# The last gate's weight rows spread more thinly over the MLP, and loaded two ahead instead of three in its second product

## The chip, the cores and the metric

The kernel runs on one core of a Trainium2 chip. The metric is the device time of one execution in microseconds, from runs on the chip; 2004.98 us is the median of three runs before the change. One more execution was profiled, and every view below is of that one.

Five engines work side by side, each through its own list of instructions and strictly in that list's order as far as this text is concerned: PE (matrix multiplication), DVE and ACT (elementwise work), POOL (here it mostly issues DMAs) and SP (it issues most DMAs). An instruction that has to wait holds everything behind it on its own engine.

## The reference, cut to what matters

One decoder layer on 512 tokens of width 2048. A conditioning vector `c` gives six modulation vectors; the sixth, `gt2`, gates the output of the MLP:

```
mod = (c_act @ w_ada[l] + b_ada[l]).reshape(B, N_MOD, D)
sh1, sc1, gt1, sh2, sc2, gt2 = [mod[:, j][:, None, :] for j in range(N_MOD)]
...
h = rmsnorm(x, g_norm_mlp[l]) * (1.0 + sc2) + sh2
hid = jnp.square(jax.nn.relu(jnp.einsum('bsd,df->bsf', h, w_mlp_in[l])))
y = jnp.einsum('bsf,fd->bsd', hid, w_mlp_out[l])
x = (x + gt2 * y)
...
return rmsnorm(x, g_norm_final)
```

`gt2` depends only on `c` and `w_ada`, so it can be computed at any time before the first finished column block of the second product is multiplied by it. `w_mlp_in` is 2048 x 8192 and `w_mlp_out` 8192 x 2048, all in float32.

## The kernel before, in words

The core first computes attention, the recurrence and their output product (up to about 780 us), and then the MLP, which is the rest.

**The MLP's two products.** Both are done as Strassen-like block products (`strassen`, L1079): seven products of blocks (`PRODUCTS`, L1073) are summed in seven PSUM banks, and `combine` (L1110 to L1117) adds and subtracts the seven banks to four result blocks. A *chunk* is one step of the inner loop: one 512 KB block of weights and 42 matmuls (L1099, L1100, L1101, 128x128 by 128x256). A *set* is the chunks that sum into the same seven banks. The first product has 15 sets of 8 chunks (g = 1 to 15; I number its chunks 0 to 119). The second has 124 chunks of this kind, 120 to 243, in 13 `parts`. PSUM has 8 banks, which the sets take in turn, so a set's first chunk finds one bank free, and the six others as soon as `combine` of the set before has read them.

**What a chunk needs.** `operands` (L1048) loads the weight block on SP into one of three `raw` buffers (L1055) and prepares it: DVE adds parts of it (L1057, L1064, L1065, into `ts`), ACT rounds both to a high part (L1063 and L1069), and DVE subtracts to get the low parts (two L122 subtractions, `w<-raw,w` with 768 columns and `w<-ts,w` with 1024). PE multiplies by the high and the low part. The buffers `w` come free when PE has done with them.

**Beside the chunks** of the first product, `keep_parts` squares and stores the four results of the set before (POOL stores at L937 and L946) for the second product. In the second, `load_pair` (L1138 `a<-part`, L1141 `a<-sum`, on SP) brings them back, `split_pair` (ACT L1148, DVE L122) splits the sums, and at the end of a part the seven banks are copied out and stored by POOL (L1289, `prod<-a`), or combined.

**The rows.** `ada_late(GT2)` (L1185) computes the gate: 64 *rows*, each a 128x512 quarter of a row block of `w_ada`, 256 KB. For each: SP loads it (L1189; the order of these loads in SP's list is kept as written), DVE multiplies it by the conditioning vector and sums along it (L1200, `SCALAR_TENSOR_TENSOR` and the `DVE_READ_ACCUMULATOR` that comes with it), and after each fourth two tiny DVE operations finish a piece (L1205, L1206). The rows run as a background job that starts with g = 2. It is paced: each chunk gives one tick, and the job goes on by one row per `pace[0]` ticks. If it is not done when the gate is first needed (`ensure(GT2)`, before the first finished column block, 108 chunks into the second product), the rest is emitted at once there. While the first product is written, the rows use the buffers `n` (5 of them, `row[0] = "n"`); from the second product on `a` (64 of them), which are also those of `load_pair` and of the copies that POOL stores.

The order of each engine's list is set by a scheduler from the order in the program and from priorities: the loads and preparations of `operands` are raised by 200 places (`SETW`), `combine` by 330 (`SETE`). So a change of the background's pace also shifts where the neighbours of a row stand.

Of the kernel before, what the change touches and what calls it, by code (L numbers as in the profile page):

```python
# [19 lines left out]
NK = D // P  # L20
# [44 lines left out]
def hybrid_layer_kernel(  # L65
# [32 lines left out]
    def T(tag, dt=F32, cols=None):  # L98
        return new(next(split_tag) if tag == "w4" else tag, dt, cols)
# [48 lines left out]
    def col(base, j):  # L148
        return vec[:, base + j : base + j + 1]
# [29 lines left out]
    def later(ins):  # L179
        return tc.keep_in_program_order(ins)  # L180


    def mod(m, j):
        return mods[:, m * NK + j : m * NK + j + 1]

    class Rows:
# [6 lines left out]
        def load(self, n, tags):  # L193
            queue = nc.sync if tags is MID else nc.sync if tags is LATE else nc.sync
            for _ in range(n):
                if self.todo and tags:
                    i, q = self.todo.pop(0)
                    t = T(next(tags))[:, :1024]
                    later(queue.dma_start(t, w_adaT[i * P : (i + 1) * P, q * 1024 : (q + 1) * 1024]))
                    self.tiles[i, q] = t  # L200
# [68 lines left out]
    class Lane:  # L269
# [8 lines left out]
        def next(self):  # L278
            if not self.queue:
                return False  # L280
            try:
                self.wait += next(self.queue[0]) or 0.0
            except StopIteration:
                self.queue.pop(0)
            return True
# [421 lines left out]
    pace = [3.2]  # L707
# [463 lines left out]
    todo = {}  # L1171
# [11 lines left out]
    LEAD, row = 3, ["n"]  # L1183

    def ada_late(m):  # L1185

        def load(i):
            t = T(row[0])
            tc.keep_in_program_order(nc.sync.dma_start(t, w_adaT[(m * NK + i // 4) * P : (m * NK + i // 4 + 1) * P, i % 4 * S : (i % 4 + 1) * S]))  # L1189
            return t  # L1190

        ts = [load(i) for i in range(LEAD)]
        for i in range(4 * NK):
            t, q = ts.pop(0), i % 4
            if i + LEAD < 4 * NK:
                ts.append(load(i + LEAD))
            yield pace[0]
            if q == 0:
                ga = T("ga")
            stt(  # L1200
                out=t, in0=t, scalar=1.0, in1=cb[q // 2][:, q % 2 * S : (q % 2 + 1) * S], op0=ALU.mult, op1=ALU.mult,
                accum_out=ga[:, q : q + 1],
            )
            if q == 3:
                tt(out=ga[:, :2], in0=ga[:, :2], in1=ga[:, 2:4], op=ALU.add)  # L1205
                stt(  # L1206
                    out=mod(m, i // 4), in0=ga[:, 0:1], scalar=ga[:, 1:2], in1=col(C_BADA, m * NK + i // 4),
                    op0=ALU.add, op1=ALU.add,
                )
        ready.add(m)  # L1210

    pace[0] = 1.9
    w_pair = w_mlp_in.rearrange("(c k p) f -> k p c f", c=2, p=P)
    for g in range(1, NG):
        if g == 2:
            bg2.add(ada_late(GT2))
        last = (lambda j: after_set()) if g == NG - 1 else None
        bs = strassen(lambda j: w_pair[j][:, :, g * 512 : (g + 1) * 512], acts_in, last, js=range(KP)[:: -1 if g == 1 else 1])
        with tc.high_priority(offset=SETE):
            r = [T("a") for _ in range(4)]  # L1220
            q11, q12, q22, q21 = combine(bs, *r)

            rs = q12, q11, q21, q22
        bg.add((keep_parts if g < NG - 2 else hold_parts)(g, *rs))
# [235 lines left out]
```

## Time and profile before

| | before |
|---|---|
| median of 3 runs | 2004.98 us (2004.24 to 2006.26) |
| the profiled execution | 2004.49 us |
| its span, first to last instruction | 2002.8 us |
| PE busy | 1947.9 us, 97% of the span |
| DVE busy | 1761.3 us, 88% |
| ACT busy | 1076.5 us, 54% |
| DMA, mean | 220 GB/s |
| the rows (L1200) | 62 in `n` from 836.4 to 1357.5 us, 2 in `a` from 1410.5 to 1414.5 us |

The first product of the MLP (chunks 0 to 119) ends at about 1356 us; the second product runs from there to the end. In a window of 40 us in which PE never waits, 355 or 356 matmuls are counted. A matmul's busy time (0.28 us) is more than the distance between two of them, since they overlap; the count per window tells the pace, and the busy time only when PE stood still. A few matmul records can be missing, so a count that is 2 short with a busy time of 40.00 is no loss.

### The profile page before, as it was taken

To read this page: it belongs to the slowest core of one execution; us is meant where nothing else is said; L and a number is where in the kernel's file an instruction comes from. 1 tells how busy PE (TensorE), PEld (TensorE's weight loads), DVE (VectorE), ACT (ScalarE), POOL (GpSimd) and SP (SyncE) were. 2 spreads that over 40 slices of the span, in tenths; PEclk is the share of its full clock that TensorE was granted. 3 is DMA by queue.
4 is the path that set the end of the run, shared out by engine and by line. 5 is a ranking of instruction groups with operands and counts; after the bars stand their busy time and mean duration, and the time that the engine had idled before them with its cause. 6 is when DMAs were issued, how large, how long until landed. Compare 5 with 4: busy or idle time off the path is not lost. (4 is left out here: it accounts for less than half of the span.)

```text
span 2002.8 us, 37929 instructions
## 1 busy us (share of the span) xinstructions
PE 1947.9 (97%) x14532; PEld 1837.3 (92%) x14532; DVE 1761.3 (88%) x2971; ACT 1076.5 (54%) x1572; POOL 181.2 (9%) x283
## 2 busy tenths in 40 slices
PE   8999999999999998999999999999999999999997
PEld 6789898788888898999999999999999999999996
DVE  8998786878998599999999999999879879788986
ACT  4443564786533385555555556556445545555542
POOL 0000000000000000112111211200110210210000
PEclk9999999999999999999999999999999999999998
DMA  9896655556779544766666666755577667677644
GB/s 364 303 318 215 207 167 184 181 150 215 226 250 369 170 139 138 233 196 213 217 193 208 227 195 193 228 177 195 185 250 252 247 246 273 229 254 272 235 148 153
DMA packets 205624, 441.45 MB, mean 220 GB/s; under 512 B 20353, under 2 KB 41985, under 8 KB 205442
## 3 DMA queue, kind: packets, MB, share of 16 engines
q1 hardware_dynamic: 178642, 360.78, 54.9%
q0 software_dynamic: 21760, 71.32, 9.5%
q10 hardware_dynamic: 5040, 6.93, 1.0%
q8 instruction: 114, 1.87, 0.4%
q14 instruction: 68, 0.56, 0.1%
HBM read 375.25 MB, written 63.70 MB: 219 GB/s over the span
## 5 line engine op out<-in xcount | busy, mean ns | idle before, releaser
L1099 PE MATMUL ps_mm<-a,w 128*128 128x256 f32 x1696 | 468.8, 277 | 2.3 <-DVE a L1111 1.2
L1101 PE MATMUL ps_mm<-a,w 128*128 128x256 f32 x1696 | 468.9, 277 | 2.1 <-DVE w L122 1.9
L1100 PE MATMUL ps_mm<-a,w 128*128 128x256 f32 x1696 | 468.8, 277 | 0.3 <-DVE a L122 0.3
L1069 ACT ACTIVATE w<-ts 128x1024 fp32r<-128x1024 f32 x244 | 258.8, 1061 | 273.9 <-DVE ts L1065 248.7
L1101 PE MATMUL ps_z<-a,w 128*128 128x256 f32 x1304 | 361.6, 278 | 8.3 <-DVE w L122 8.3
L1099 PE MATMUL ps_z<-a,w 128*128 128x256 f32 x1304 | 361.5, 278 | 3.6 <-DVE a L1115 1.6
L1100 PE MATMUL ps_z<-a,w 128*128 128x256 f32 x1304 | 361.1, 277 | 0.1
L122 DVE TENSOR_TENSOR w<-ts,w 128x1024 fp32r<-128x1024 f32 x244 | 298.6, 1224 | 58.6 <-PE ps_mm L1101 26.5
L1099 PEld LDWEIGHTS ps_mm<-a,w 128*128 128x128 f32 x1696 | 318.6, 188 | 3.6 <-issue 2.5
L1101 PEld LDWEIGHTS ps_mm<-a,w 128*128 128x128 f32 x1696 | 318.9, 188 | 2.9 <-DVE w L122 2.8
L1100 PEld LDWEIGHTS ps_mm<-a,w 128*128 128x128 f32 x1696 | 319.0, 188 | 0.7 <-DVE a L122 0.7
L122 DVE TENSOR_TENSOR w<-raw,w 128x768 fp32r<-128x768 f32 (+1 forms) x296 | 268.5, 909 | 39.0 <-ACT w L244 23.6
L1063 ACT ACTIVATE w<-raw 128x768 fp32r<-128x768 f32 x244 | 204.8, 840 | 169.8 <-issue 85.5
L1101 PEld LDWEIGHTS ps_z<-a,w 128*128 128x128 f32 x1304 | 245.4, 188 | 10.0 <-DVE w L122 9.9
L1099 PEld LDWEIGHTS ps_z<-a,w 128*128 128x128 f32 x1304 | 245.7, 188 | 5.0 <-issue 2.1
L1100 PEld LDWEIGHTS ps_z<-a,w 128*128 128x128 f32 x1304 | 245.8, 189 | 0.6 <-DVE a L122 0.6
L244 ACT ACTIVATE wh<-wr 128x512 fp32r<-128x512 f32 (+1 forms) x184 | 113.4, 620 | 152.3 <-PE ps_mm L262 65.2
L259 PE MATMUL ps_mm<-a,wh 128*128 128x512 f32 x448 | 176.2, 393 | 3.7 <-DVE a L460 1.6
L1057 DVE TENSOR_TENSOR ts<-raw 128x512 f32<-128x512 f32 x244 | 167.8, 688 | 12.8 <-DMA raw<-in_w_mlp_out_dram 11.9
L263 PE MATMUL ps_mm<-a,wl 128*128 128x512 f32 x448 | 175.1, 391 | 0.4 <-DVE wl L122 0.2
L262 PE MATMUL ps_mm<-a,wh 128*128 128x512 f32 x448 | 174.8, 390 | 0.0
L122 DVE TENSOR_TENSOR wl<-wr,wh 128x512 fp32r<-128x512 f32 (+1 forms) x184 | 124.7, 681 | 33.3 <-ACT wh L244 32.5
(332 smaller groups left out, 4154.4 us busy)
## 6 DMA issues: line engine op xcount, KB each, us to landing
raw<-in_w_mlp_out_dram SPq DMA_DIRECT2D x124, 512.0 KB, 4.2
raw<-in_w_mlp_in_dram SPq DMA_DIRECT2D x120, 512.0 KB, 3.9
x<-in_w_adaT_dram SPq DMA_DIRECT2D x108, 512.0 KB, 5.8
wr<-in_w_in_dram SPq DMA_DIRECT2D x160, 256.0 KB, 3.4
tt<-in_w_adaT_dram SPq DMA_DIRECT2D x52, 512.0 KB, 6.5
part<-a POOLq DMA_DIRECT2D x84, 256.0 KB, 3.9
a<-part SPq DMA_DIRECT2D x84, 256.0 KB, 6.4
prod<-a POOLq DMA_DIRECT2D x63, 256.0 KB, 5.8
```

The source lines that it names most:

```text
L122: tt(out=out, in0=full, in1=f32(high), op=ALU.subtract)
L244: act(h[:, :n], r[:, :n], AF.Copy)
L259: first = mm(out, wh, ah, start=start, stop=False, **kw)
L262: mm(out, wh, al, start=False, stop=False, **kw)
L263: mm(out, wl, ah, start=False, stop=stop, **kw)
L1057: tt(out=t[:, : 2 * HT].rearrange("p (a b) -> p a b", a=2), in0=r[:, HT : 3 * HT].rearrange("p (a b) -> p a b", a=2), in1=r[:, q_(0)].unsq ...
L1063: act(h, r[:, HT:], AF.Copy)
L1069: act(h, t, AF.Copy)
L1099: mm(out, wh[:, blk(i)], ah, start=st, stop=False, **kw)
L1100: mm(out, wh[:, blk(i)], al, start=False, stop=False, **kw)
L1101: mm(out, wl[:, blk(i)], ah, start=False, stop=j == js[-1], **kw)
```

## The change

The pace goes from 1.9 ticks per row to 3.2. The loads are kept in a list, `todo`; while the rows use the buffers `n`, three of them are ahead of the row that is computed, as before, and once they use `a`, two.

```diff
-        ts = [load(i) for i in range(LEAD)]
+        todo = list(range(4 * NK))
+        ts = [load(todo.pop(0)) for _ in range(LEAD)]
         for i in range(4 * NK):
             t, q = ts.pop(0), i % 4
-            if i + LEAD < 4 * NK:
-                ts.append(load(i + LEAD))
+            if todo and len(ts) < (LEAD if row[0] == "n" else 2):
+                ts.append(load(todo.pop(0)))
             yield pace[0]
...
-    pace[0] = 1.9
+    pace[0] = 3.2
```

64 rows at 1.9 ticks take 122 ticks, and 112 chunks are left of the first product when the job starts. At 3.2 they take 205 ticks, of 112 + 108 before the gate is needed. In the lists of the engines, DVE's rows stand before: 60 by chunk 113, then one each near chunks 121 and 122, 132 and 133. They stand now: 37 by chunk 112, one at 121, and 26 between chunks 132 and 203. In pieces: six rows at chunks 20 to 24 before and six now, six at 31 to 33 before and two at 31 and 32 now, 34 in the sets from chunk 48 to 111 before and 20 now.

The lists also change around the end of the first product. On ACT, which copies the first of the seven banks of the last set (L1110), before:

```order
1111 L1063 ACTIVATE w_2731_15908<-raw_15904 128x768
1112 L1069 ACTIVATE w_2733_15914<-ts_15906 128x1024
1113 L1063 ACTIVATE w_2742_15981<-raw_15977 128x768
1114 L1110 ACTIVATE a_15766<-ps_z_15224 128x512
1115 L1069 ACTIVATE w_2744_15987<-ts_15979 128x1024
```

and after:

```order
1111 L1063 ACTIVATE w_2701_15818<-raw_15814 128x768
1112 L1069 ACTIVATE w_2703_15824<-ts_15816 128x1024
1113 L1110 ACTIVATE a_15679<-ps_z_15142 128x512
1114 L1063 ACTIVATE w_2711_15886<-raw_15882 128x768
1115 L1069 ACTIVATE w_2713_15892<-ts_15884 128x1024
```

`raw_15977` before and `raw_15882` after are the same weights, those of chunk 122. The copy of the bank stood behind the rounding of these weights, and stands now ahead of it.

On DVE at the same place, where the rest of `combine` (L1111 and on) frees the other banks, before:

```order
1912 L1057 TENSOR_TENSOR ts_15979<-raw_15977 128x512
1913 L1200 SCALAR_TENSOR_TENSOR n_15698,ga_16117<-n_15698,cb_81 128x512
1914 L1064 TENSOR_TENSOR ts_15979<-ts_15979,raw_15977 128x256
1915 L1065 TENSOR_TENSOR ts_15979<-ts_15979,raw_15977 128x256
1916 L122 TENSOR_TENSOR w_2734_15915<-ts_15906,w_2733_15914 128x1024
1917 L1111 TENSOR_TENSOR a_15768<-ps_mm_15225,a_15766 128x512
1918 L122 TENSOR_TENSOR w_2743_15982<-raw_15977,w_2742_15981 128x768
1919 L1112 TENSOR_TENSOR a_15766<-ps_mm_15226,a_15766 128x512
1920 L1113 TENSOR_TENSOR a_15769<-ps_mm_15227,a_15768 128x512
```

and after:

```order
1877 L1057 TENSOR_TENSOR ts_15884<-raw_15882 128x512
1878 L1064 TENSOR_TENSOR ts_15884<-ts_15884,raw_15882 128x256
1879 L1065 TENSOR_TENSOR ts_15884<-ts_15884,raw_15882 128x256
1880 L1111 TENSOR_TENSOR a_15681<-ps_mm_15143,a_15679 128x512
1881 L122 TENSOR_TENSOR w_2704_15825<-ts_15816,w_2703_15824 128x1024
1882 L1112 TENSOR_TENSOR a_15679<-ps_mm_15144,a_15679 128x512
1883 L1113 TENSOR_TENSOR a_15682<-ps_mm_15145,a_15681 128x512
```

One row (L1200) is gone from between, and L1111 stands one low part earlier; it still stands behind L1057, which needs the weights of chunk 122.

On SP, early in the second product, the loads of rows now stand between those of weights; from the weights of chunk 131 (`raw_16460`) on, after the change:

```order
661 L1055 DMA raw_16460<-in_w_mlp_out_dram 128x2x512
662 L1189 DMA a_16203<-in_w_adaT_dram 128x512
663 L1189 DMA a_16402<-in_w_adaT_dram 128x512
664 L1055 DMA raw_16516<-in_w_mlp_out_dram 128x2x512
665 L1189 DMA a_16573<-in_w_adaT_dram 128x512
666 L1055 DMA raw_16575<-in_w_mlp_out_dram 128x2x512
667 L1055 DMA raw_16631<-in_w_mlp_out_dram 128x2x512
668 L1055 DMA raw_16687<-in_w_mlp_out_dram 128x2x512
669 L1189 DMA a_16746<-in_w_adaT_dram 128x512
```

A row's load waits for the work that last used its buffer `a`. For 11 of the rows in the second product that is a store of POOL's (L1289, `prod<-a`) which has to land first.

## The prediction

> **What bounds the kernel now.** I read the page's busy times first, then the MLP in windows of 40 us, then who made PE wait in the windows that fall short.
>
> ```profile
> PE 1947.9 (97%) x14532; PEld 1837.3 (92%) x14532; DVE 1761.3 (88%) x2971; ACT 1076.5 (54%) x1572; POOL 181.2 (9%) x283
> ```
>
> PE is the bound over the whole, so only what makes PE stand still can be won. The windows say where it does (columns: window, its length, busy time and count of PE, PEld, DVE, ACT and POOL, PE's granted clock, DMA share, GB/s):
>
> ```profile
> 880.00:920.00 40.00, 38.73 (x334) 37.98 (x333) 39.15 (x74) 20.01 (x28) 7.50 (x11) 1.00 0.70 220
> 920.00:960.00 40.00, 38.91 (x333) 37.99 (x332) 39.79 (x72) 21.10 (x29) 6.85 (x10) 1.00 0.62 200
> 960.00:1000.00 40.00, 40.00 (x355) 40.00 (x355) 39.34 (x67) 22.57 (x30) 6.86 (x10) 1.00 0.65 206
> ...
> 1080.00:1120.00 40.00, 39.76 (x350) 39.59 (x350) 38.88 (x68) 21.90 (x29) 6.85 (x10) 1.00 0.64 202
> ...
> 1160.00:1200.00 40.00, 39.41 (x345) 39.08 (x344) 39.69 (x67) 22.80 (x30) 6.85 (x10) 1.00 0.63 202
> ...
> 1240.00:1280.00 40.00, 39.83 (x347) 39.40 (x345) 38.69 (x70) 21.21 (x29) 8.20 (x12) 1.00 0.65 209
> 1280.00:1320.00 40.00, 39.40 (x344) 39.22 (x345) 39.37 (x69) 22.64 (x31) 8.21 (x12) 1.00 0.67 220
> 1320.00:1360.00 40.00, 37.70 (x328) 37.13 (x326) 38.12 (x61) 23.77 (x33) 0.00 (x0) 1.00 0.60 202
> 1360.00:1400.00 40.00, 38.74 (x311) 37.78 (x312) 38.13 (x62) 24.86 (x38) 0.56 (x1) 0.96 0.47 160
> 1400.00:1440.00 40.00, 40.00 (x355) 40.00 (x355) 35.60 (x58) 20.43 (x27) 5.91 (x11) 1.00 0.51 168
> ...
> 1480.00:1520.00 40.00, 40.00 (x356) 40.00 (x355) 33.53 (x51) 21.95 (x30) 2.19 (x4) 1.00 1.04 387
> ...
> 1640.00:1680.00 40.00, 40.00 (x356) 40.00 (x354) 36.96 (x57) 23.31 (x31) 0.00 (x0) 1.00 1.01 367
> ```
>
> A full window has 355 matmuls, so one is 40 / 355 = 0.113 us, and each missing one costs that. The six windows of the first product that fall short miss 21, 22, 5, 10, 8 and 11: 77 x 0.113 = 8.7 us. The two at the change from the first to the second product miss 27 + 44 = 71: 8.0 us. From 1400 us on the second product is full. And DVE: 39 of 40 us in the first product, where PE falls short, and 33 to 37 of 40 in the second, where it does not. Who makes PE wait:
>
> ```profile
> PE ps_z L1099 <- DVE a L1115: 0.5, 1, 0.5
> PE ps_o L1099 <- DVE a L1111: 0.5, 1, 0.5
> ...
> PE ps_z L1099 <- ACT a L1110: 1.5, 1, 1.5
> ...
> PE ps_mm L1099 <- DVE a L1111: 1.2, 1, 1.2
> PE ps_mm L1100 <- DVE a L122: 0.3, 1, 0.3
> ```
>
> The first two are of 880 to 920 us, the third of 1340 to 1360, the last two of 1360 to 1380. Nearly all are L1110 to L1116, `combine`, for the first matmul of a product (L1099): the set waits for a bank that DVE has yet to read. `combine` stands among the preparations of weights on an engine that is 98% busy, so it comes as late as DVE runs behind. That is my reading: the losses at set starts are DVE's backlog.
>
> **The change, part by part.** What a row costs and where it lies (L1200 alone: busy time and count of DVE; then the groups of that line):
>
> ```profile
> 880.00:920.00 40.00, 4.90 (x14) 1.00 0.70 220
> 920.00:960.00 40.00, 4.90 (x14) 1.00 0.62 200
> 960.00:1000.00 40.00, 2.79 (x8) 1.00 0.65 206
> ...
> L1200 DVE SCALAR_TENSOR_TENSOR n<-n,cb x62: 683/692/701, 836.4 to 1357.5; 128x512 f32<-128x512 f32 x62
> ```
>
> Each row counts twice (the operation and the reading of its sum), so the two windows with the largest losses hold seven rows, and the next, with four, holds none. A row occupies DVE for less than its 692 ns, since operations overlap. The place at the change of products shows it, DVE first, then ACT, then SP's issue of the weights that both then wait for:
>
> ```profile
> 1356.89 0.69 DVE L1057 TENSOR_TENSOR ts<-raw 128x512 f32<-128x512 f32 x1 [1.57 <-DMA raw<-in_w_mlp_out_dram]
> 1357.50 0.68 DVE L1200 SCALAR_TENSOR_TENSOR n<-n,cb 128x512 f32<-128x512 f32 x1
> ...
> 1358.11 0.42 DVE L1064 TENSOR_TENSOR ts<-ts,raw 128x256 f32<-128x256 f32 x1
> ...
> 1358.91 1.22 DVE L122 TENSOR_TENSOR w<-ts,w 128x1024 fp32r<-128x1024 f32 x1
> 1360.05 0.68 DVE L1111 TENSOR_TENSOR a<-ps_mm,a 128x512 f32<-128x512 f32 x1
> ...
> 1356.90 0.84 ACT L1063 ACTIVATE w<-raw 128x768 fp32r<-128x768 f32 x1 [2.43 <-DMA raw<-in_w_mlp_out_dram]
> 1357.65 0.58 ACT L1110 ACTIVATE a<-ps_z 128x512 f32<-128x512 f32 x1
> ...
> 1350.03 0.47 SPq L1055 DMA_DIRECT2D raw<-in_w_mlp_out_dram  x1
> ```
>
> From 1357.50 to 1358.11 is 0.61 us for a row.
>
> *Rows taken out of the first product.* 62 rows before, 38 after (37 by chunk 112 and one at 121): 24 x 0.61 = 14.6 us of DVE work leave a stretch of some 520 us. PE wins only what it lost there, at most 8.7 us. Which set starts? The new order has six rows at chunks 20 to 24, as the old one has, so the window of 880 to 920 us (2.4 us, around the start of chunk 24) stays. Chunk 32's start (920 to 960 us, 2.5 us) has two rows in front of it instead of six: I take 2.2 of the 2.5. The later four windows lost 3.8 us with 34 rows in the sets from chunk 48 to 111; 20 are left, so a set is relieved by 14 / 8 x 0.61 = 1.1 us, while the largest wait among them is half of that (below). I take all 3.8. Sum: **6.0 us**, between 0 (rival two) and 8.7.
>
> ```profile
> PE ps_mm L1099 <- DVE a L1115: 0.6, 1, 0.6
> ```
>
> *The change of products.* Its 8.0 us begin with the late weights of chunk 122: SP issued them at 1350.03, behind ten loads of stored parts, and ACT and DVE waited 2.43 and 1.57 us for them. Behind that wait stood ACT's copy of the first bank (L1110), hence PE's 1.5 us, and DVE's L1111, hence 1.2. In the new order L1110 stands ahead of those weights, so the 1.5 goes for certain. L1111 still stands behind L1057, L1064 and L1065, but without the row (0.61) and one low part (1358.91 to 1360.05, 1.14 us); and with DVE less behind, the whole chain of loads starts earlier against PE, since SP's loads wait for a `raw` buffer that DVE must have read. 0.61 + 1.14 cover the 1.2 and the 0.3. So 3.0 us of waits go. The clock falls with them:
>
> ```profile
> 1360.00:1364.00 4.00, 3.13 (x15) 3.16 (x15) 4.00 (x8) 1.89 (x5) 0.00 (x0) 0.61 0.72 254
> ```
>
> At 0.61 for 4 us, 4 x 0.39 = 1.6 us more are lost; the shorter waits at other set starts left the clock at 1.00, so I let it go too. The other 3.4 us of the 8.0 are small losses spread over chunks 122 to 127, which I leave. Sum: **4.6 us**, between 1.5 and 8.0. The Trainium skill ("TensorE: Matmul & The Clock Gate", Part 1, The HAM clock gate) has the clock halve after an idle window of about 3.4 us; the trace disagrees, as 1.5 + 1.2 us of waiting with work between were enough for 0.61. By the page the 1.6 us would not hang on these waits, and the sum would be 3.0.
>
> *Rows put into the second product.* 26 instead of 2: 24 x 0.61 = 14.6 us of DVE work over chunks 132 to 203, some 340 us, in which DVE has 3 to 8 us in 40 to spare and waits for PE to free its buffers:
>
> ```profile
> DVE w L122 <- PE ps_mm L1101: 7.6, 7, 1.1
> ...
> DVE ts L1057 <- DMA raw<-in_w_mlp_out_dram: 4.3, 3, 2.2
> DVE w L122 <- PE ps_mm L1101: 1.9, 2, 1.1
> ...
> DVE ts L1057 <- DMA raw<-in_w_mlp_out_dram: 1.9, 2, 1.0
> ```
>
> The first is of 1440 to 1480 us: there a row costs nothing, as PE's own pace covers it. The others are of 1480 to 1520 and 1640 to 1680, where the DMA engines are full (1.04 and 1.01), DVE waits for weights, and an added row costs twice: 0.61 us on DVE and 256 KB at 387 or 367 GB/s, 0.68 or 0.71 us of DMA. Three rows fall on each. First stretch: 3 x 1.29 = 3.9 us, of which the 1.9 that DVE waits for PE are cover; second: 3 x 1.32 = 4.0, against 40 - 36.96 - 1.9 = 1.1 us of cover. At worst 2.0 + 2.9 = 4.9 us. Below nothing it can't go, since no wait is taken out there. The cover of the chunks on both sides counts too, and the loads are small beside the 15.5 MB of such a window (387 GB/s x 40 us), so I take **1 us**.
>
> *Two loads ahead instead of three.* It takes one buffer `a` of 64 less and puts a load one row, 3.2 chunks of 42 x 0.113 = 4.7 us, later. Two rows ahead are still over 25 us, against the landing times of these loads:
>
> ```profile
> DMA to landing us min/median/max: 3.4/4.2/9.9
> ```
>
> So nothing on DVE's side. On SP's side a row waits with the weights behind it; that is rival three.
>
> Sum: -6.0 - 4.6 + 1.0 = -9.6 us on the profiled execution's 2004.49: 1994.9. The median is 0.5 above that execution, so the **forecast is 1995.4 us**.
>
> **The rivals.** *One, everything comes back:* DVE's relief empties all windows up to 1400 us, 8.7 + 8.0 = 16.7 us, and the second product hides its rows: 2004.98 - 16.7 = 1988.3. For it: from 960 to 1000 us, with four rows in the window, PE was full. Against it: the rows at chunks 20 to 24 stay, and the loads ahead of chunk 122's weights are all still there.
>
> *Two, DVE's total is not what delays `combine`:* set starts wait because `combine` stands behind certain preparations, which the pace does not alter. For it: DVE was busy for 39.34 us from 960 to 1000 us, where nothing was lost, and for 38.69 from 1240 to 1280, where 0.9 was. Then only the 1.5 us of L1110 and some of L1111 go, and the second product takes 1 back: 2004.98 - 3 + 1 = 2003.0, no change that can be told. Against it: the match of rows and losses above.
>
> *Three, slower: SP.* A row's load stands in SP's list ahead of weights, and 11 of them wait for a store of POOL's to land.
>
> ```profile
> prod<-a POOLq DMA_DIRECT2D x63, 256.0 KB, 5.8
> ...
> 1485.07 0.56 SPq L1055 DMA_DIRECT2D raw<-in_w_mlp_out_dram  x1
> ...
> 1494.69 0.38 SPq L1055 DMA_DIRECT2D raw<-in_w_mlp_out_dram  x1
> ```
>
> Weights were already 9.6 us apart in the full stretch, twice a chunk's 4.7. If two such loads in each of the two stretches hold SP for a store's 5.8 us, the weights come 2 x 11.6 = 23.2 us later, less 1.9 + 1.1 of cover: 20.2 lost, 10.6 won before, so 2004.98 + 9.6 = 2014.6. It decides as soon as SP stands still for longer than that cover with DVE waiting for weights. Against it: outside these stretches three `raw` buffers keep weights several chunks ahead, and POOL stored only 4 and 0 times in the two windows (its counts above).
>
> *Four, the upper bound of the rows' cost* in the second product, 4.9 instead of 1: 1995.4 + 3.9 = 1999.3.
>
> The Trainium skill ("DMA: Bandwidth & Descriptors", Specifications) gives about 358 GB/s from HBM to one core; the 387 GB/s of the window at 1480 us is above that, so the trace disagrees. By the page a row there would cost 0.73 us of DMA instead of 0.68, and the upper bound 5.1.
>
> **How the numbers follow.** Forecast 0.56, rival one 0.11, rival two 0.16, rival three 0.09, rival four 0.08. From no change this kernel's measurement tells about 0.2%, 4.0 us, so faster is below 2001.0: forecast, one and four, 0.75; within 0.2%: two, 0.16; slower: three, 0.09. The forecast's own range is 1990.5 to 2000. The range for 8 in 10 leaves out most of rival one below and rival three above, and reaches to rival two: 1989.0 to 2003.0.
>
> **What would show it.** Right: the windows between 920 and 1320 us (with the clock of the changed kernel) at 40.00 us of PE; 880 to 920 as before; no wait of PE for L1110 at the change of products and the clock there near 1.00; L1200's counts at three or four rows per 40 us up to 1770 us; full windows of PE throughout. Wrong: PE waiting in the second product for DVE L122 or for weights between 1400 and 1760 us, SP's gaps between weights over 10 us there, or set starts that still wait for L1111 to L1116 with DVE below 38 of 40.

## The result, and the profile after

The changed kernel takes 2008.91 us (median of 12 runs, 2003.66 to 2012.96), the kernel before 2004.96 in the runs beside it. The ratio is 1.002, with a 95% interval of 1.0011 to 1.0029: slower by about 4 us, where 9.6 less were forecast. The profiled execution took 2008.65 us, against 2004.49 before.

The windows of 40 us that answer to those shown of before (window, length, busy time and count of PE, PEld, DVE, ACT, POOL, PE's clock, DMA share, GB/s):

```profile
880.00:920.00 40.00, 39.42 (x343) 38.93 (x343) 39.01 (x68) 20.99 (x29) 6.82 (x10) 1.00 0.59 188
920.00:960.00 40.00, 39.76 (x352) 39.59 (x351) 39.50 (x68) 22.19 (x30) 6.85 (x10) 1.00 0.61 193
...
1160.00:1200.00 40.00, 40.00 (x355) 40.00 (x354) 38.52 (x63) 23.15 (x32) 6.85 (x10) 1.00 0.59 185
...
1280.00:1320.00 40.00, 40.00 (x355) 40.00 (x355) 39.51 (x68) 22.40 (x30) 8.20 (x12) 1.00 0.64 206
1320.00:1360.00 40.00, 38.93 (x339) 38.47 (x339) 37.92 (x61) 24.45 (x35) 0.00 (x0) 1.00 0.71 244
1360.00:1400.00 40.00, 39.81 (x336) 38.94 (x336) 39.62 (x63) 23.63 (x33) 3.77 (x7) 1.00 0.50 168
...
1480.00:1520.00 40.00, 36.63 (x299) 36.43 (x298) 33.62 (x54) 19.61 (x26) 0.00 (x0) 0.91 0.93 318
...
1640.00:1680.00 40.00, 37.58 (x316) 37.33 (x316) 32.38 (x55) 20.56 (x28) 0.00 (x0) 0.96 0.92 313
1680.00:1720.00 40.00, 37.82 (x327) 37.19 (x327) 34.66 (x58) 21.41 (x31) 6.52 (x12) 1.00 0.72 246
```

The set starts of the first product and the change of products are better, as forecast. But three windows of the second product that were full before are not: 299, 316 and 327 matmuls instead of 355 or 356. Two long windows hold the account. Before:

```profile
840.00:1400.00 560.00, 552.47 (x4794) 547.86 (x4794) 548.23 (x940) 310.60 (x415) 87.42 (x128) 1.00 0.64 205
1400.00:1840.00 440.00, 440.00 (x3884) 440.00 (x3884) 367.57 (x542) 235.94 (x310) 54.27 (x100) 1.00 0.68 241
```

and after:

```profile
840.00:1400.00 560.00, 557.92 (x4891) 555.93 (x4891) 546.20 (x896) 318.11 (x423) 90.65 (x134) 1.00 0.62 199
1400.00:1840.00 440.00, 431.94 (x3758) 430.67 (x3757) 365.75 (x580) 227.27 (x297) 49.41 (x91) 0.99 0.71 247
```

At 0.113 us for a matmul, 97 more up to 1400 us are 11.0 us won, and 126 fewer from 1400 to 1840 us are 14.2 us lost. That is 3.2 of the 4.2 us between the two profiled executions. Both traces hold all 42 matmuls of each of the 244 chunks, so the account can also be made from the start of each chunk's first matmul: 7.9 us are won in chunks 16 to 114 and 3.1 in 115 to 130 (chunk 120 takes 6.5 us instead of 9.6), and 14.4 are lost in 131 to 227. The last microsecond isn't the rows': chunk 3 already starts at 785.2 us instead of 784.1, and the first load of a row is issued at 796.1. The traces of all runs differ by up to 2.9 us in the start of chunk 0 alone.

Who waits, from 1400 to 1840 us, DVE first and then PE (engine and line, who ended the wait: us in total, times, longest), after the change:

```profile
DVE a L1201 <- DMA a<-in_w_adaT_dram: 21.7, 9, 8.3
...
PE ps_mm L1101 <- DVE w L122: 3.7, 2, 2.4
PE ps_o L1101 <- DVE w L122: 3.4, 1, 3.4
PE ps_z L1099 <- ACT ps_z L1089: 0.9, 1, 0.9
```

L1201 is the row's operation (L1200 before). DVE stands 21.7 us for the data of nine rows, and PE then stands for the low parts that are queued behind: 3.4 us in chunk 147 and 2.4 in chunk 180. These two chunks lose 10.7 of the 14.4 us. The rest isn't shown to be of this kind: chunk 190 loses 1.6 us, where DVE had waited 2.1 us for ACT and then done two rows whose data were there, and chunk 192 loses 1.4, 0.9 of it waiting for a bank that ACT fills (L1089). ACT had stood for a stored sum shortly before chunk 190 (1680 to 1720 us):

```profile
ACT a L1148 <- DMA a<-sum: 4.6, 2, 3.7
```

The place of the longest wait, on SP and then on DVE and PE:

```profile
1474.14 0.37 SPq L1189 DMA_DIRECT2D a<-in_w_adaT_dram  x1
...
1475.21 0.43 DVE L1065 TENSOR_TENSOR ts<-ts,raw 128x256 f32<-128x256 f32 x1
1483.93 0.69 DVE L1201 SCALAR_TENSOR_TENSOR a<-a,cb 128x512 f32<-128x512 f32 x1 [8.29 <-DMA a<-in_w_adaT_dram]
1484.55 0.08 DVE L1201 DVE_READ_ACCUMULATOR a<-a,cb 128x1 f32 x1
1484.55 1.22 DVE L122 TENSOR_TENSOR w<-ts,w 128x1024 fp32r<-128x1024 f32 x1
...
1485.82 0.58 PE L1101 MATMUL ps_o<-a,w 128*128 128x256 f32 x1 [3.37 <-DVE w L122]
```

The row's load was issued at 1474.14. DVE had reached its operation at about 1475.6 and stood until 1483.93: 9.8 us from issue to use, in a stretch with the DMA engines full of stored parts. The L122 behind is the low part that PE needs for the chunk under way. Chunk 147, which lasted 11.2 us instead of 4.8, alone cost 6.4 us: 3.4 of standing, the rest a halved clock (in windows of 1 us it is 0.50 from 1485 to 1491 us):

```profile
1484.00:1488.00 4.00, 2.18 (x10) 2.18 (x11) 3.93 (x7) 0.00 (x0) 0.00 (x0) 0.61 1.02 371
1488.00:1492.00 4.00, 4.00 (x22) 4.00 (x22) 3.62 (x6) 1.13 (x2) 0.00 (x0) 0.54 0.93 312
```

The Trainium skill ("TensorE: Matmul & The Clock Gate", Part 1, The HAM clock gate) has the clock halve after about 3.4 us without work. Here the trace agrees (3.37 us, then 0.54); the clock of 0.61 at the change of products before, after 1.5 and 1.2 us of waiting, shows that less can be enough.

So "two loads ahead" is not what the engines' lists hold. The scheduler put the operation into DVE's list right behind its load on SP: 18 of the 25 operations on rows in `a` stand in DVE's list ahead of even the first step (L1057) of the weight block that SP issues last before the row's load, and four more behind that step, ahead of the next block's. All nine operations that waited are among the 18. That count can be made in the lists before any run, and I hadn't made it.

### The profile page after: what moved, and what is told of

It is laid out like the page before. It is cut to its first block, busy times and chain, and to the rows that moved or that the text cites. A ratio compares the mean times of both kernels' runs of the same rounds, so it can differ in the third digit from the quotient of the medians.

```text
span 2006.9 us, 37948 instructions
## 1 busy us (share of the span) xinstructions
PE 1949.7 (97%) x14532; PEld 1839.1 (92%) x14532; DVE 1759.9 (88%) x2971; ACT 1077.7 (54%) x1572; POOL 181.2 (9%) x283
## 4 chain that ended last, share of the span: by engine, by line
issue 41%; PE 33%; DVE 9%; DMA 9%; POOL 5%; ACT 2%; SPq 1%; POOLq 0%; DVEq 0%; ACTq 0%
PE ps_mm L259 4%; PE ps_mm L263 4%; PE ps_mm L262 4%; POOL part L937 3%; DVE w L122 2%; POOL sum L946 2%; PE ps_z L259 2%; PE ps_z L263 2%; PE ps_z L262 2%; PE ps_mm L1101 2%; PE ps_mm L1100 2%; PE ps_mm L1099 1%; DMA x<-in_w_adaT_dram 1%; PE ps_z L1099 1%; PE ps_z L1101 1%
## 5 line engine op out<-in xcount | busy, mean ns | idle before, releaser
L122 DVE TENSOR_TENSOR w<-ts,w 128x1024 fp32r<-128x1024 f32 x244 | 298.3, 1223 | 43.3 <-PE ps_mm L1101 19.3
L122 DVE TENSOR_TENSOR w<-raw,w 128x768 fp32r<-128x768 f32 (+1 forms) x296 | 268.1, 908 | 46.4 <-ACT w L244 24.3
L1057 DVE TENSOR_TENSOR ts<-raw 128x512 f32<-128x512 f32 x244 | 167.5, 687 | 6.1 <-DMA raw<-in_w_mlp_out_dram 5.6
L211 DVE SCALAR_TENSOR_TENSOR x<-x,cb 128x1024 f32<-128x1024 f32 x108 | 131.7, 1223 | 27.5 <-DMA x<-in_w_adaT_dram 22.9
```

The source lines that it names most:

```text
L122: tt(out=out, in0=full, in1=f32(high), op=ALU.subtract)
L211: ins = stt(out=t, in0=t, scalar=1.0, in1=cb[q_], op0=ALU.mult, op1=ALU.mult, accum_out=self.ga[:, q_ : q_ + 1],)
L1057: tt(out=t[:, : 2 * HT].rearrange("p (a b) -> p a b", a=2), in0=r[:, HT : 3 * HT].rearrange("p (a b) -> p a b", a=2), in1=r[:, q_(0)].unsq ...
```

## The experiments

Each is timed against the kernel before, in the same session. Theory W is that DVE waits for rows whose data have yet to land; theory T, that the rows' loads take the place of weights and stored parts; theory D, that DVE can't carry the added work.

**Holding the operation to its place.** `later` keeps an instruction in program order, as the loads already were:

```diff
-            stt(
+            ins = stt(
                 out=t, in0=t, scalar=1.0, in1=cb[q // 2][:, q % 2 * S : (q % 2 + 1) * S], op0=ALU.mult, op1=ALU.mult,
                 accum_out=ga[:, q : q + 1],
             )
+            if row[0] == "a":
+                later(ins)
```

> The changed kernel, with the row's operation on DVE held to its place in the program during the second product; its loads stay where they are on SP. In DVE's list the operation then stands 6 to 19 chunks behind its load instead of at most 1. Theory W (in the second product the row's operation reaches the head of DVE's list before its data have landed, 21.7 us of such waits in the profile of the changed kernel, and the low parts stand behind it): these waits fall to under 1 us, the 14.2 us that PE lost between 1480 and 1720 us fall to some 3, and the time is about 1995 to 1998. Theory T (the rows' loads take SP's and the DMA engines' time from the weights and the stored parts): PE loses some 10 us or more there all the same and the time stays at 2006 to 2009. Theory D (24 more rows are too much work for DVE in the full stretches): the loss stays too, since the work is the same.

2005.11 us, ratio 1.0003 (0.9994 to 1.0012). The waits for rows in `a` are gone entirely, and the two stretches with full DMA engines are full of matmuls:

```profile
1480.00:1520.00 40.00, 40.00 (x355) 40.00 (x355) 34.76 (x59) 22.05 (x30) 0.00 (x0) 1.00 1.01 370
...
1640.00:1680.00 40.00, 40.00 (x355) 40.00 (x355) 36.69 (x61) 22.75 (x31) 0.00 (x0) 1.00 1.03 375
```

But the time was expected at 1995 to 1998, and new losses stand elsewhere, at the starts of parts (chunks 160, 168, 176, 192, 200). The waits of ACT, then of PE, in this kernel from 1400 to 1840 us:

```profile
ACT a L397 <- DMA prod<-a: 10.0, 6, 2.2
...
PE ps_o L1099 <- ACT ps_o L1089: 2.6, 1, 2.6
PE ps_z L1099 <- ACT ps_z L1089: 1.9, 3, 0.7
```

L397 is ACT's copy of a bank at a part's end, into a buffer `a`; it waits for a store of an earlier copy, from the buffer that it got, to land. I take it that no other buffer was free. Behind it on ACT stands L1089, which brings the next part's stored sum into a bank, and PE waits for that. Hence theory B: a held row keeps its buffer `a` for 6 to 12 chunks, three at a time, and the ends of parts then run out of buffers. In the changed kernel, with the same loads but no row held, the list of ACT's waits has none of L397 for a store.

**The loads without the operations.**

```diff
+            if row[0] == "a":
+                if q == 3:
+                    nc.vector.memset(mod(m, i // 4), 1.0)
+                continue
```

> The changed kernel, but of the rows that use the buffers of the second product only the load is left: nothing is computed of them, and the gate's pieces that they would give are set to 1 (left out: part of the last gate). Theory T: the loss of 14.2 us in the second product stays, time 2006 to 2009. Theories W and D: it goes nearly whole, time 1993 to 1997. Against the run with the held operations it tells what DVE's work itself costs there: by D some 5 to 10 us, by W under 2.

1995.75 us, ratio 0.9959 (0.9947 to 0.9972). The second product is full again:

```profile
1400.00:1840.00 440.00, 440.00 (x3884) 440.00 (x3884) 363.11 (x531) 235.42 (x310) 54.32 (x100) 1.00 0.72 258
```

All the loads are there, at the same places of SP's list among the weights, and cost nothing: T falls. (Nothing reads a row here, so its buffer need not be kept, and the run says nothing on the buffers.)

**Each part of the change alone.** The pace alone (`pace[0] = 3.2`, three ahead in both products):

> The kernel before with the pace 3.2 alone: three loads ahead in both products. All theories: if the number of loads ahead mattered as I took it to (one row more is three chunks more), W would expect waits of DVE for rows near 0 and a time of 1995. But in SP's and DVE's lists of this kernel each row's operation still stands right behind its load, one row earlier only, so W as I hold it now expects the same as of the changed kernel: waits of some 20 us, 2006 to 2010.

2008.37 us, 1.0011 (1.0000 to 1.0022). The waits are those of the changed kernel:

```profile
DVE a L1200 <- DMA a<-in_w_adaT_dram: 23.9, 9, 8.1
```

One load more ahead doesn't shorten them, since the operation moves up with its load. Two ahead, at the old pace of 1.9:

> The changed kernel with the old pace of 1.9: two loads ahead in the second product, where two rows of 64 lie. Expected by all theories: as before, 2003 to 2007, within 0.2% of it.

2004.32 us, 0.9998 (0.9989 to 1.0007): nothing, as expected. So the loss comes with the pace.

**The held operations without loads.** The rows' data left out, the operation works on one tile for good:

```diff
         def load(i):
+            if row[0] == "a":
+                return rest[0]
             t = T(row[0])
+            rest[0] = t
```

> The kernel with the held operations, but the rows of the second product are not loaded (left out: their data; the operation runs in place on one tile that has been there since the first product, so the last gate's values are not the reference's). Theory B (what the held kernel loses at the starts of parts, some 0.9 us at chunks 160, 168, 176, 192 and 5.9 at 200 and 201, comes from the buffers a: a row that waits for ten chunks keeps one, and ACT's copy at a part's end then waits for a buffer whose store has yet to land): no row has such a buffer here, so these losses are gone and the time is 1994 to 1998. Theory D (DVE's work itself, 24 x 0.61 us, is what the second product can't carry): the losses stay, 2002 or more.

2023.03 us, 1.0093 (1.0078 to 1.0109), a miss by 25 us. The tile that I kept was one of the five buffers `n`, and through these the stored sums of a part come back. The waits of ACT and of PE from 1400 to 1840 us show it:

```profile
ACT ps_z L1089 <- DMA n<-prod: 11.1, 5, 2.7
ACT ps_mm L1089 <- DMA n<-prod: 8.2, 4, 2.8
...
PE ps_z L1099 <- ACT ps_z L1089: 7.2, 4, 2.8
PE ps_mm L1099 <- ACT ps_mm L1089: 4.9, 3, 3.2
```

The run said nothing on B or D. Done again with the tile in `a`, one of 64:

> As the run of held operations without loads, but the one tile on which they run is of the buffers a instead of n (of which that run kept one of five for good, so that the stored products of a part, which come back through n, came late). Left out again: the data of 24 rows. B: one buffer of 64 gone, no loss at the starts of parts above 2 us, 1994 to 1998. D (DVE's work): 2002 or more.

1997.99 us, 0.9968 (0.9955 to 0.9980), and the second product full:

```profile
1400.00:1840.00 440.00, 440.00 (x3884) 440.00 (x3884) 378.90 (x601) 235.00 (x310) 54.26 (x100) 1.00 0.69 243
```

All of DVE's work on rows is in it, 378.90 us busy against 363.11 without the operations, and PE loses nothing: D falls.

**How many rows are held.** The held operations with one load ahead (`... else 1` in place of 2), with three, and with none (the row is loaded one pace before its operation):

> The kernel with the held operations, but one load ahead instead of two in the second product: a row's buffer is kept 3 to 9 chunks instead of 6 to 12, and two are kept instead of three. Theory B: the losses at the starts of parts shrink from 9.6 us to 3 to 6, time 1998 to 2002, with still no wait of DVE for a row. If the number of loads ahead is not what counts there, 2003 to 2007 as before it.

> The kernel with the held operations and three loads ahead in the second product instead of two (one ahead: 1995.35 us, two: 2005.11). Theory B (rows that are kept long take the buffers a that ACT's copies at a part's end need): ACT's waits in L397 for stores, 3.9 us with one ahead and 10.0 with two, grow to 15 or more, PE's losses at the starts of parts to 12 to 25 us, time 2008 to 2020. Against B: no further growth, 2003 to 2007.

> The kernel with the held operations and no load ahead in the second product: each row is loaded one pace before its operation, and stands in DVE's list 0 to 6 chunks behind its load instead of 3 to 9. By W and B together: ACT's waits for stores at a part's end fall below 2 us, but at the rows that stand less than two chunks behind their load (six of 25) DVE waits for data again, 3 to 10 us in all; time 1995 to 2001, no better than one ahead.

| held, loads ahead | ratio (interval) | L397 waiting for stores, us (times) | matmuls 1400 to 1840 us |
|---|---|---|---|
| three | 1.0020 (1.0008 to 1.0032) | 17.1 (12) | 3766 |
| two | 1.0003 (0.9994 to 1.0012) | 10.0 (6) | 3801 |
| one | 0.9963 (0.9949 to 0.9977) | 3.9 (4) | 3873 |
| none | 0.9964 (0.9951 to 0.9977) | none | 3867 |

The rows of the waits view for three, of ACT and of DVE, and the second product's window for one:

```profile
ACT a L397 <- DMA prod<-a: 17.1, 12, 3.2
...
DVE a L399 <- DMA prod<-a: 17.1, 7, 4.0
...
1400.00:1840.00 440.00, 439.31 (x3873) 438.92 (x3872) 378.38 (x602) 235.56 (x308) 54.12 (x100) 1.00 0.72 256
```

The waits for a buffer rise with the rows that are kept, and the lost matmuls with them (118, 83, 11 of 3884): B holds. The table has ACT's copies alone; DVE makes the others (L399) and waits for stores too, 17.1 us with three and 1.3 with two, and not at all with one or none. With none ahead I expected DVE to wait 3 to 10 us for data again. No such wait is listed: the shortest time from the issue of a row's load to its operation was 8.6 us there. And 17 matmuls (1.9 us) are missing at another place, chunk 216, where PE waits for a low part. One ahead is 1995.35 us: it **beats both kernels**, and the 1998 to 2002 that I expected. In its trace no row in `a` is waited for.

**One ahead, but not held:**

> The changed kernel with one load ahead instead of two in the second product, the row's operations not held. In DVE's list each operation still stands at most one chunk behind its load. Theory W: DVE waits some 15 to 25 us for rows as in the changed kernel, time 2005 to 2010. If what made the run with held operations and one ahead fast is the one buffer less alone, this one is at 1995 to 1999 as well.

2008.88 us, 1.0022 (1.0010 to 1.0035), with 23.6 us of waits for rows:

```profile
DVE a L1201 <- DMA a<-in_w_adaT_dram: 23.6, 11, 8.6
```

So it is the holding that wins, and one load ahead only together with it.

**Other paces,** held and one ahead:

> As the last, with a pace of 2.5: the rows end at chunk 169 instead of 214, so that 4 starts of parts instead of 9 see a row's buffer, and the first product has 48 rows instead of 38. Theory B: the loss in the second product falls to 1 to 3 us; the first product's set starts give back 1 to 3 of what they won, time 1997 to 2001, faster than both kernels.

> As the last, with a pace of 2.2: rows end at chunk 150. Theory B: 0.5 to 2 us lost in the second product, 2 to 5 given back in the first; time 1997 to 2002. If the relief of DVE in the first product is not proportional to the rows but comes with the first few taken out, this one is as fast as the pace of 2.5 or faster.

2001.25 us (0.9989, 0.9978 to 0.9999) and 2000.23 us (0.9990, 0.9980 to 1.0000): faster than before by little, at the edge of what the interval tells, and slower than the pace of 3.2. From 840 to 1400 us PE runs 4867 and 4860 matmuls, against 4887 at 3.2: 20 and 27 x 0.113 = 2.3 and 3.1 us are lost again where the rows went back. Most of the relief comes with the first rows taken out, then: against the 4794 of before, 66 matmuls are won with 54 rows in `n`, 73 with 48 and 93 with 39, where 62 stood before. The medians differ from that at 3.2 by some 5 and 6 us; the rest I can't place, and the profiled executions don't show it (1999.31 us at 3.2, 2000.68 at 2.5, 1997.43 at 2.2).

## Why the prediction was wrong

*Rows taken out of the first product: right.* Forecast 6.0 us. The six short windows missed 77 matmuls before; of these windows, only that of 880 to 920 (12) and of 920 to 960 us (3) still miss any: 62 x 0.113 = 7.0 us won. Of the window that I left unchanged, nearly half was won too; its rows stand at the same chunks, and why it improved was not tested. The rival that DVE's total doesn't delay `combine` forecast no such gain, and more was won the more rows were taken out (the three paces above). But the pace moves the rows' neighbours in the lists too, and DVE is still busy for 38.5 to 39.5 us of 40 in these windows. That it is the rows' time, and not the order, was not tested apart.

*The change of products: right, but smaller.* Forecast 4.6 us; 36 more matmuls from 1320 to 1400 us are 4.1, and by chunks it is 3.1. PE's wait for L1110 is gone and the clock stays at 1.00 in 1360 to 1400 us, as foretold. The waits of PE in the changed kernel from 1320 to 1400 us have one of 0.9 us for L1112 in its place, and 0.2 for L1111 are left of 1.2:

```profile
PE ps_mm L1099 <- DVE a L1112: 0.9, 1, 0.9
```

Together 11.0 us won against 10.6. That the sum is so near is partly luck, since one term was too small and the other too large.

*Rows put into the second product: wrong, 14.2 us instead of 1,* and outside its bound of 4.9 (4.8 before its terms are rounded). The sign named for being wrong came: PE waits for DVE's L122 there. I priced the DVE time and the DMA time of a row and set them against DVE's slack. Taken singly, both are hidden: with all the loads and no operations, and with all the operations and no loads, PE loses nothing. The cost was in neither alone, but for the most part in the wait between the two.

*Two loads ahead: this is the step that failed.* I wrote that a load lies over 25 us ahead of its operation, so that "nothing on DVE's side" follows. That is the order of the program. In the engines' lists the operation stands right behind its load, and at the longest wait 9.8 us until the data were there met 1.5 us of lead. The longest landing, 9.9 us, was quoted in that very step, and the profile of before had six waits of rows, 2.9 us in all, at the same short distance; there the DMA engines were at 0.6 to 0.7, and the rows landed in time or nearly.

The same step put the buffers at a gain, "one buffer `a` of 64 less", against three loads ahead. But before, only two rows used `a` at all. The run with the held operations is the change as I had taken it to be, two loads ahead and each operation at its place in the program, 38 to 73 us behind the issue of its load. It has no wait for a row, and yet its ratio is 1.0003 (0.9994 to 1.0012): 83 matmuls, 9.4 us, go at the starts of parts, by theory B to the wait for buffers. So this step had two costs wrong, the lead and the buffers, and mending the first alone doesn't give the forecast.

*The rivals.* The third had the sign and the place, the two full stretches, but not the mechanism: SP held by stores, weights late. The loads at their places on SP cost nothing (the run without operations), and DVE waited less for weights from 1400 to 1840 us, not more; before, and then after the change:

```profile
DVE ts L1057 <- DMA raw<-in_w_mlp_out_dram: 9.5, 8, 2.2
```

```profile
DVE ts L1057 <- DMA raw<-in_w_mlp_out_dram: 2.8, 4, 1.5
```

What was late was the rows' own data.

With the operation held and only one load ahead, a kernel that the prediction did not consider, the ratio is 0.9963, 7.4 us (4.6 to 10.2) less, where 9.6 were forecast for two ahead.

## What to carry to other kernels

Distance in the program is not distance in an engine's list: where a scheduler orders the lists, a prefetch may end up with hardly any lead, and only the lists show it. On an engine that works in order, an unimportant background operation that waits for a DMA stalls everything that is queued behind it, so it must stand as far behind its load as the longest landing of a full stretch, not the median. And a lead is paid for in buffers: hold no more than the landing needs, and look at who else takes from the same pool.

## What the runs showed of the hardware

The rows' loads of the changed kernel land in 4.4 us as a median, and the slowest in 9.7 (its line's view; then the DMA issues from 1474 to 1484 us, with KB and us to landing):

```profile
DMA to landing us min/median/max: 3.4/4.4/9.7
```

```profile
raw<-in_w_mlp_out_dram SPq DMA_DIRECT2D x1, 512.0 KB, 10.7
...
a<-in_w_adaT_dram SPq DMA_DIRECT2D x1, 256.0 KB, 9.7
```

Among full DMA engines a 256 KB load took 9.7 us, and one of 512 KB 10.7. And one stall of 3.37 us of PE cost 6.4 us: the granted clock was 0.61 and 0.54 in the two windows of 4 us at and behind its end, and 1.00 before and after.
